# Convolution sums of the vector engine in PSUM, the shifting mean behind the projections, and matmul inputs placed like the weights modulo 128 bytes

## The chip, the cores and the metric

The kernel runs on one core of one Trainium2 chip. The time is that of one execution on the device in microseconds (us); the median of 3 runs is compared. The engines are named as in the profile: PE is TensorE (matmuls; PEld are its weight loads), DVE is VectorE, ACT is ScalarE, POOL is GpSimd, SP issues DMAs.

## The reference

A decoder trunk of two layers over 512 tokens of width 1024, float32. Layer 0 is an mLSTM mixer, layer 1 a Conformer convolution module; each is followed by a gated MLP (width 2816) with a depthwise convolution of three taps. The change sits in layer 1, and in where matmul inputs lie in memory.

```python
def conformer_conv_mixer(x, w_in, b_in, dw_w, dw_b, ln_g, ln_b, w_out, b_out):
    a = x @ w_in + b_in
    u = a[..., :D_MODEL] * jax.nn.sigmoid(a[..., D_MODEL:])
    u = causal_dwconv(u, dw_w, dw_b)          # 31 taps
    u = jax.nn.silu(layernorm(u, ln_g, ln_b))
    return u @ w_out + b_out

def conv_ffn(x, w_up, conv_w, conv_b, w_down):
    hdn = causal_dwconv(x @ w_up, conv_w, conv_b)
    return (jax.nn.silu(hdn[..., :D_FF]) * hdn[..., D_FF:]) @ w_down

def reference(...):
    for i in range(DEPTH):
        h = rmsnorm(x, norm_mix[i])
        x = x + (mlstm_mixer(h, ...) if i % 2 == 0 else conformer_conv_mixer(h, ...))
        x = x + conv_ffn(rmsnorm(x, norm_ffn[i]), ...)
    return rmsnorm(x, norm_final)
```

## The kernel before

Activations lie with channels on the 128 partitions and 512 tokens along the free axis, in 8 blocks of channels. Every float32 operand of a large product is split into two parts of a shorter format, high and low, and a product is done as three matmuls (`mm3`, L160 to L163): high by high, high by low, low by high. Weights come in units of 128x1024: SP loads one (`wr`), ACT writes the high part (`wh`, L149), DVE the low part (`wl`, L150). There are four buffers of `wr` and three each of `wh` and `wl`. A projection of one block is 24 matmuls of 512 columns.

The order on each engine is set when the kernel is built: a scheduler with a timeline of its own places the instructions, and each engine then runs its list strictly in that order. An instruction that waits holds up all that stand behind it on its engine.

A norm's row factor is worked out while the first projections of the next stage run (`norm_finish`, two hooks): a mean over channels on PE (`ms<-ch`, `ms<-cl`, L227 and L228), row values on DVE, the power -0.5 on POOL (`rs`, L232), then DVE spreads it over diagonals (`dgr`, L215) and PE sums those (L218) into all partitions; ACT copies the result to `rsb`. Products are multiplied by `rsb` when they leave PSUM.

In layer 1, `glu(j)` makes two projections for block j of channels (`pa`, `pb`), DVE multiplies both by `rsb` (L717, L718), ACT takes the sigmoid (L719), and DVE forms `u` (L722 or L727). The 31 taps are shared out by block: DVE does blocks 0, 2 and most of 4 (80 taps, `dve_tap`, L744), POOL block 1 and nine taps of 4 (L741, each on a product that ACT makes, L739), and PE blocks 3, 5, 6, 7 with Toeplitz matrices (`conv_pe`, L776). POOL builds those matrices (`toe`, L755; four instructions for each block, two sets of buffers), and DMAs carry `u` and the result to and from PE's layout. DVE's and POOL's taps wait in queues; `background(NV, NG)` takes up to NV and NG of them after each projection.

Then comes the layer norm. All values are shifted by the mean of block 3 (`shift`, giving `kb`), and `stats(j, e)` subtracts `kb` from block j and adds the values and their squares to the sums `s1` and `s2` (L822 to L827). PE sums these over channels (L240), and after the row factors the normalized values go to `zht` and `zlt`, the inputs of the out projection. `PLAN` says after which block which of these runs. PSUM has eight banks of 512 columns: six for `bank()`, two for `small()`.

Of the kernel before, what the change touches and what calls it, by code (L numbers as in the profile page):

```python
# [9 lines left out]
F32 = mybir.dt.float32  # L10
# [4 lines left out]
P = 128  # L15
# [5 lines left out]
NH = 4  # L21
# [5 lines left out]
NEG = -1.0e30  # L27
NPH = 4                    # token phases of the convolution on the tensor engine
NTAU = T // NPH
NJ = (CK + 2 * NPH - 3) // NPH  # L30
GR = 68                    # rows: input gates at 0, running maximum at 32, forget gates at 64

# column offsets in the packed per-channel parameter array
_COLS = {}
# [11 lines left out]
def hybrid_trunk(ctx, tc, x_in, par_in, tph_in, wg_in, wv_in, wqk_in, wo_in, mout_in, cin_in,  # L46
# [6 lines left out]
    wsp = ctx.enter_context(tc.tile_pool(name="wsp", bufs=3))  # L53
    work = ctx.enter_context(tc.tile_pool(name="work", bufs=1))
    psum = ctx.enter_context(tc.tile_pool(name="psum", bufs=6, space=bass.MemoryType.PSUM))
    psms = ctx.enter_context(tc.tile_pool(name="psms", bufs=2, space=bass.MemoryType.PSUM))
# [12 lines left out]

# [1 line left out]
    par = const.tile([P, NPAR], F32, name="par")  # L71
# [22 lines left out]
    def warm(n, after=None):  # L94
        """Products that nobody reads, to keep the clock of the tensor engine up over a wait."""
        ps = bank()
        for _ in range(n):
            with tc.issue_after(after.ins) if after is not None else nullcontext():
                after = PE.matmul(ps[:, :P], ones, ones, start=True, stop=True)  # L99

# [1 line left out]
    seq = []  # L102
# [61 lines left out]

# [1 line left out]
    xh = [None] * KD  # L166
# [31 lines left out]
    def to_rows(src, c, tag):  # L198
        """Values along the free axis, equal on all partitions -> [128 tokens, blocks]."""
        nb = (c.stop - c.start) // P  # L200
        dg = work.tile([P, T], F32, tag="tmp", name=nm("dg"), bufs=4)
        V.tensor_tensor(out=blocks(dg, c), in0=src,
                        in1=ident[:].unsqueeze(1).to_broadcast([P, nb, P]), op=ALU.mult)
        r4 = work.tile([P, NTB], F32, tag=tag, name=nm(tag))
        V.tensor_reduce(out=r4[:, :nb], in_=blocks(dg, c), op=ALU.add, axis=mybir.AxisListType.X)
        return r4

    def from_rows(r4, nb, pb):
        """[128 tokens, blocks] -> the values along the free axis on all partitions (PSUM)."""
        hl = work.tile([P, 2, NTB], F32R, tag="hl", name=nm("hl"))  # L210
        V.tensor_copy(hl[:, 0, :nb], r4[:, :nb])
        V.tensor_tensor(out=hl[:, 1, :nb], in0=r4[:, :nb], in1=hl[:, 0, :nb], op=ALU.subtract)
        for i in range(2):
            dg = work.tile([P, NTB, P], F32R, tag="tmp", name=nm("dgr"), bufs=4)
            v = V.tensor_tensor(out=dg[:, :nb], in0=ident[:].unsqueeze(1).to_broadcast([P, nb, P]),  # L215
                            in1=hl[:, i, :nb].bitcast(F32).unsqueeze(2).to_broadcast([P, nb, P]),
                            op=ALU.mult)
            p = PE.matmul(pb, onesr, dg[:, :nb].rearrange("p a b -> p (a b)"), start=i == 0, stop=i == 1)  # L218
        return v, p

    def col_mean(ps, t, c, w):
        """Sum over the partitions of t times the constant in w, on all partitions."""
        h = work.tile([P, T], F32R, tag="tmp", name=nm("ch"), bufs=4)
        l = work.tile([P, T], F32R, tag="tmp", name=nm("cl"), bufs=4)
        A.copy(h[:, c], t[:, c])
        V.tensor_tensor(out=l[:, c], in0=t[:, c], in1=h[:, c], op=ALU.subtract)
        PE.matmul(ps, w, h[:, c], start=True, stop=False)  # L227
        PE.matmul(ps, w, l[:, c], start=False, stop=True)  # L228
# [6 lines left out]
    def row_sums(ps, t, c, w, start, stop):  # L235
        """Adds the sums over the partitions of t, times w, to ps: [128 tokens, 2 * blocks]."""
        nb = (c.stop - c.start) // P
        for b in range(nb):
            s = slice(c.start + b * P, c.start + (b + 1) * P)
            PE.matmul(ps[:, 2 * b : 2 * b + 2], t[:, s], w[:, :2], start=start and b == 0,  # L240
                      stop=stop and b == nb - 1)

    def norm_rows(nrm, c):
        """1 / rms of the tokens in c, [128 tokens, blocks]."""
        n = c.stop - c.start
# [6 lines left out]

    # the row factors of a norm are worked out between the first products of the next stage
    hooks = []
# [19 lines left out]

    # ================= layer 0: mLSTM =================
    warm(9)
# [47 lines left out]
    VW = DV + 2  # L324
    vh = [mp.tile([P, NTB, VW], F32R, tag=f"vgh{h}", name=f"vh{h}") for h in range(NH)]
    vl = [mp.tile([P, NTB, VW], F32R, tag=f"vgl{h}", name=f"vl{h}") for h in range(NH)]
    for h in range(NH):
# [29 lines left out]

    # gates, channel-major: input gates on partitions 0-3, forget gates on 32-35
    wgh, wgl = next_unit()
# [81 lines left out]
    def att_decay(h):  # L441
        """exp of the decay from s to t less the running maximum; s on partitions, t free."""
        plf, pm = small(), small()
# [147 lines left out]

    # ================= gated MLP with a depthwise convolution =================
    def ffn(l, g=None, last=False):
# [98 lines left out]

    # ================= layer 1: convolution module =================
    cctx = ExitStack()
    cp = cctx.enter_context(tc.tile_pool(name="conv", bufs=1))
    DVE_CH, POOL_CH, PE_CH = (0, 2, 4), (1,), (3, 5, 6, 7)
    NV, NG, NG4, NPRE = 5, 4, 9, 1
    cacc2 = cp.tile([P, T], F32, name="caccp")
# [4 lines left out]
    cacc = {c: cp.tile([P, T], F32, name=f"cacc{c}") for c in range(8)}  # L703
    # 1 where the partition lies in the block of NPH partitions
    tph = cp.tile([P, 8 * 4 * NJ * NPH], F32, name="tph")
# [31 lines left out]
    def pool_tap(j, u, s):  # L737
# [3 lines left out]
        G.tensor_tensor(out=a[:, s:], in0=a[:, s:], in1=p[:, s:], op=ALU.add)  # L741

    def dve_tap(j, u, s):
        V.scalar_tensor_tensor(out=cacc[j][:, s:], in0=u[:, : T - s],  # L744
                               scalar=dw(j, CK - 1 - s), in1=cacc[j][:, s:],
                               op0=ALU.mult, op1=ALU.add)

# [36 lines left out]

    # taps for the vector engine and GpSimd, handed out between the products
    vtaps, gtaps = [], []
# [13 lines left out]
    def shift():  # L800
        """The mean of one block of channels, by which all values are shifted before their sums."""
        d[FIRST] = cp.tile([P, T], F32, name=f"d{FIRST}")
# [10 lines left out]
    def stats(j, e):  # L813
        if j in PE_CH:
# [3 lines left out]
                in0=cacc[j].rearrange("p (q t) -> p t q", q=NPH), scalar=pcol("dw_b", j),  # L818
                in1=kb.rearrange("p (t q) -> p t q", q=NPH), op0=ALU.add, op1=ALU.subtract)
        else:  # L820
            d[j] = cacc[j]
# [9 lines left out]
        5: [lambda: conv_pe(3, *us[3])],  # L831
        6: [shift],
        13: [lambda: stats(1, G)],
        14: [lambda: stats(0, V), lambda: stats(5, V)],
# [3 lines left out]
    for j in range(8):  # L838
# [3 lines left out]
        else:  # L842
            conv_start(j, u)
            if j == 4:
# [7 lines left out]
        for f in PLAN.get(j, ()):  # L852
            f()
    for j in PE_CH[1:]:
        background(2 * NV, 2 * NG)
        conv_pe(j, *us[j])
        for f in PLAN.get(j + 8, ()):
            f()
    background(999, 999)
    G.tensor_tensor(out=cacc[4], in0=cacc[4], in1=cacc2, op=ALU.add)  # L860
    sq4 = stats(4, V)
    sq7 = stats(LAST, None)

    # layer norm over channels
    pr1, pr2, pmu = small(), small(), bank()
# [36 lines left out]
def _layout(inputs):  # L902
    f = {k: np.asarray(v) for k, v in inputs.items()}

    def ch(a):  # [..., C] -> [128, ... * C/128], channel c = m * 128 + p
        a = a.reshape(a.shape[:-1] + (-1, P))
        return np.moveaxis(a, -1, 0).reshape(P, -1)

    def taps(w):  # [K, C] -> [128, C/128 * K]
        k, c = w.shape  # L910
        return w.reshape(k, c // P, P).transpose(2, 1, 0).reshape(P, -1)

    def cols(w, n=P):  # [K, N] -> [N/n, 128, K/128 * n]
        k, c = w.shape
        return w.reshape(k // P, P, c // n, n).transpose(2, 1, 0, 3).reshape(c // n, P, -1)

    # gate biases: input gates on partitions 0-3, forget gates on 32-35
    bg = np.zeros((P, 1), np.float32)
    bg[0:4, 0], bg[32:36, 0] = f["m_b_gates"][0][:4], f["m_b_gates"][0][4:]
    # taps by token phase: dph[c * NPH + p, m, g, j, q] = w[K - 1 - (NPH * j + q - p), m * 128 + g * 32 + c]  # L920
    dw = f["c_dw_w"][0].reshape(CK, KD, 4, P // 4)
# [52 lines left out]
```

## Time and profile before

| | |
|---|---|
| median of 3 runs (lowest, highest) | 1192.71 us (1192.66, 1192.79) |
| span of the profiled execution, first to last instruction | 1191.0 us |
| PE busy, matmuls | 1134.3 us (95%), 5226 |
| DVE busy | 788.6 us (66%), 1022 |
| ACT busy | 510.8 us (43%), 713 |
| POOL busy | 174.8 us (15%), 126 |
| mean granted TensorE clock | 0.974 |

The profiled execution has no time of its own beside its span. The span is 1.7 us below the median, and this is what lies around it in a run. A matmul's duration is that of its whole way through the pipeline; the distance from one start to the next tells how fast PE goes. Busy DVE instructions overlap their neighbours by some 0.08 us where nothing holds them.

### The profile page before, as it was taken

What the parts mean: (1) busy time and instruction counts of PE and PEld (TensorE: products, weight loads), DVE (VectorE), ACT (ScalarE), POOL (GpSimd) and SP (SyncE); (2) the same over time, 40 slices, a digit from 0 to 9 for tenths busy, and PEclk for the clock granted to TensorE, in tenths of its full rate; (3) what the DMA queues carried; (4) which work ended last, traced back from release to release, by engine and by line L of the source; (5) the groups of instructions that cost most, each with busy time, mean ns of one, the idle gap of its engine ahead of it and who ended that gap; (6) DMA issues with size and microseconds to landing.
All of it is one profiled execution on the core that took longest, in us unless ns stands there. A gap on an engine that the chain in (4) does not pass through costs nothing.

```text
span 1191.0 us, 13476 instructions
## 1 busy us (share of the span) xinstructions
PE 1134.3 (95%) x5226; PEld 939.7 (79%) x5226; DVE 788.6 (66%) x1022; ACT 510.8 (43%) x713; POOL 174.8 (15%) x126
## 2 busy tenths in 40 slices
PE   9999999999999999999998757699999999999996
PEld 7788888888888888888887647588888888888886
DVE  6788875487777775332479999874877777752222
ACT  6556774354444443222244522363544444432221
POOL 4000001100000000000267857021000000000002
PEclk9999999999999999999998879699999999999998
DMA  6222123223232323233332112022232323233322
GB/s 247 89 89 71 54 74 103 90 89 106 89 106 89 105 86 92 90 97 98 110 105 62 62 44 67 14 88 89 92 103 90 106 89 106 84 98 89 93 62 71
DMA packets 36369, 106.85 MB, mean 90 GB/s; under 512 B 4049, under 2 KB 10321, under 8 KB 36305
## 3 DMA queue, kind: packets, MB, share of 16 engines
q1 hardware_dynamic: 31728, 103.25, 27.2%
q10 hardware_dynamic: 4576, 2.74, 0.8%
q8 instruction: 41, 0.67, 0.2%
q14 instruction: 24, 0.19, 0.0%
HBM read 101.78 MB, written 2.10 MB: 87 GB/s over the span
## 4 chain that ended last, share of the span: by engine, by line
PE 84%; DVE 13%; issue 1%; ACT 1%; DMA 1%; POOL 0%; ACTq 0%; POOLq 0%; SPq 0%; DVEq 0%
PE mm L161 25%; PE mm L162 25%; PE mm L163 25%; DVE cacc L744 8%; PE mm L580 2%; PE mm L577 2%; PE mm L576 2%; DVE wl L150 2%; PE ms L240 1%; PE mm L99 0%; DMA xall<-in_dram 0%; PE ms L218 0%; DVE u L722 0%; DVE se L453 0%; DVE s L826 0%
## 5 line engine op out<-in xcount | busy, mean ns | idle before, releaser
L163 PE MATMUL mm<-xh,wl 128*128 128x512 f32 x960 | 375.6, 391 | 3.3 <-DVE wl L150 3.3
L161 PE MATMUL mm<-xh,wh 128*128 128x512 f32 x960 | 375.6, 392 | 0.0
L162 PE MATMUL mm<-xl,wh 128*128 128x512 f32 x960 | 375.4, 391 | 0.0
L150 DVE TENSOR_TENSOR wl<-wr,wh 128x1024 fp32r<-128x1024 f32 (+1 forms) x192 | 236.5, 1235 | 165.5 <-ACT wh L149 163.3
L149 ACT CAST wh<-wr 128x1024 fp32r<-128x1024 f32 (+1 forms) x192 | 197.4, 1030 | 296.1 <-PE mm L162 243.6
L163 PEld LDWEIGHTS mm<-xh,wl 128*128 128x128 f32 x960 | 181.4, 189 | 41.9 <-DVE wl L150 3.7
L162 PEld LDWEIGHTS mm<-xl,wh 128*128 128x128 f32 x960 | 181.4, 189 | 37.9
L161 PEld LDWEIGHTS mm<-xh,wh 128*128 128x128 f32 x960 | 181.5, 189 | 37.2
L193 POOL TENSOR_TENSOR acc<-acc,sq 128x512 f32<-128x512 f32 x30 | 43.3, 1444 | 746.7 <-ACT sq L191 746.2
L161 PE MATMUL mm<-yh,wh 128*128 128x512 f32 (+1 forms) x374 | 142.3, 380 | 0.0
L162 PE MATMUL mm<-yl,wh 128*128 128x512 f32 (+1 forms) x374 | 142.3, 380 | 0.0
L163 PE MATMUL mm<-yh,wl 128*128 128x512 f32 (+1 forms) x374 | 142.2, 380 | 0.0
L606 DVE TENSOR_TENSOR mm<-mm,rsb 128x512 f32<-128x512 f32 x88 | 60.8, 695 | 76.0 <-PE mm L163 73.1
L744 DVE SCALAR_TENSOR_TENSOR cacc<-u,par,cacc 128x501 f32<-128x501 f32 (+27 forms) x80 | 102.1, 1321 | 0.1
L161 PEld LDWEIGHTS mm<-yh,wh 128*128 128x128 f32 x374 | 70.0, 187 | 15.5
L162 PEld LDWEIGHTS mm<-yl,wh 128*128 128x128 f32 x374 | 70.0, 187 | 15.3
L163 PEld LDWEIGHTS mm<-yh,wl 128*128 128x128 f32 x374 | 70.0, 187 | 15.2
L616 ACT CAST yh<-ta 128x512 fp32r<-128x512 f32 x44 | 27.3, 620 | 104.6 <-DVE ta L615 104.6
L611 DVE SCALAR_TENSOR_TENSOR ta<-mm,par,ta 128x511 f32<-128x511 f32 x88 | 65.6, 745 | 1.3
L611 DVE SCALAR_TENSOR_TENSOR tb<-mm,par,tb 128x511 f32<-128x511 f32 x88 | 65.5, 746 | 1.4
L614 ACT ACTIVATE ta<-ta 128x512 f32<-128x512 f32 x44 | 27.8, 632 | 79.4 <-DVE ta L611 79.4
L741 POOL TENSOR_TENSOR cacc<-cacc,cprod 128x511 f32<-128x511 f32 (+29 forms) x30 | 49.5, 1651 | 24.1 <-ACT cprod L739 22.4
(237 smaller groups left out, 1200.5 us busy)
## 6 DMA issues: line engine op xcount, KB each, us to landing
wr<-in_dram SPq DMA_DIRECT2D x175, 512.0 KB, 3.5
wr<-in_dram SPq DMA_DIRECT2D x16, 384.0 KB, 3.1
xall<-in_dram SPq DMA_DIRECT2D x8, 256.0 KB, 6.4
us<-u ACTq DMA_DIRECT2D x16, 64.0 KB, 2.1
out_dram<-xall SPq DMA_DIRECT2D x2, 384.0 KB, 3.5
tph<-in_dram SPq DMA_DIRECT2D x1, 576.0 KB, 4.5
wr<-in_dram SPq DMA_DIRECT2D x2, 256.0 KB, 3.9
cacc<-co ACTq DMA_DIRECT2D x8, 64.0 KB, 2.4
```

The lines of the kernel that those rows point to most:

```text
L149: st["last"] = A.copy(hi[:, :n], r[:, :n])
L150: V.tensor_tensor(out=lo[:, :n], in0=r[:, :n], in1=hi[:, :n], op=ALU.subtract)
L161: PE.matmul(ps, lh, rh, start=start, stop=False)
L162: PE.matmul(ps, lh, rl, start=False, stop=False)
L163: PE.matmul(ps, ll, rh, start=False, stop=stop)
L193: e.tensor_tensor(out=nrm.acc[:, c], in0=nrm.acc[:, c], in1=sq[:, c], op=ALU.add)
L606: V.tensor_tensor(out=ps, in0=ps, in1=rs["b"], op=ALU.mult)
L611: V.scalar_tensor_tensor(out=t[:, s:], in0=ps[:, : T - s], scalar=pcol("fconv_w", m * 3 + 2 - s), in1=t[:, s:], op0=ALU.mult, op1=ALU.add)
L614: A.activation(ta, ta, AF.Silu)
L616: A.copy(yh[:, j, :], ta)
L741: G.tensor_tensor(out=a[:, s:], in0=a[:, s:], in1=p[:, s:], op=ALU.add)
L744: V.scalar_tensor_tensor(out=cacc[j][:, s:], in0=u[:, : T - s], scalar=dw(j, CK - 1 - s), in1=cacc[j][:, s:], op0=ALU.mult, op1=ALU.add)
```

## The change

Four things change; all else in the diff is comments.

1. `dve_tap` accumulates in a PSUM bank. At a block's first tap a bank is taken and ACT writes the first term there; after the last one ACT copies the sum to `cacc[j]` (for block 4, DVE's `stats` reads the bank and adds `cacc2`, from which POOL has taken `kb` before). In a tap one input is `u` in SBUF, the other and the output are in the bank. NV is 4, not 5.
2. `shift` goes from after block 6 to after block 7, with POOL's `stats(1)`; `conv_pe(5)` comes up from behind the projections to after block 6.
3. A tile `pad` of 64 bytes stands at the head of the pool `work`, which moves every tile behind it.
4. The mLSTM's `v` tiles, whose places the mixer's outputs take over later, are made 96 bytes longer.

In the built program, tiles start at these bytes of a partition modulo 128. Weights `wh` and `wl`, and the norm outputs `xh` and `xl`: 64 before and after. The MLP's `yh` and `yl`, and the layer norm's `zht` and `zlt`: 0 before, 64 after. The mixer's `gh` and `gl`: 0, 32, 64 and 96 for heads 0 to 3 before, 64 for all after. Modulo 512 they agree less: the weights are at 64, `yh` and `yl` go from 256 to 320, `zht` and `zlt` from 128 to 192.

```diff
-    DVE_CH, POOL_CH, PE_CH = (0, 2, 4), (1,), (3, 5, 6, 7)
-    NV, NG, NG4, NPRE = 5, 4, 9, 1
+    NV, NG, NG4, NPRE = 4, 4, 9, 1
...
+    work.tile([P, 16], F32, name="pad")
...
-    vh = [mp.tile([P, NTB, VW], F32R, tag=f"vgh{h}", name=f"vh{h}") for h in range(NH)]
+    def v_tile(what, h):
+        t = mp.tile([P, NTB * VW + 24], F32R, tag=f"vg{what}{h}", name=f"v{what}{h}")
+        return t[:, : NTB * VW].rearrange("p (a b) -> p a b", a=NTB)
+    vh = [v_tile("h", h) for h in range(NH)]
...
+    pacc = {}
+
     def dve_tap(j, u, s):
-        V.scalar_tensor_tensor(out=cacc[j][:, s:], in0=u[:, : T - s],
-                               scalar=dw(j, CK - 1 - s), in1=cacc[j][:, s:],
-                               op0=ALU.mult, op1=ALU.add)
+        if j not in pacc:
+            pacc[j] = bank()
+            A.activation(pacc[j], u, AF.Identity, scale=dw(j, CK - 1), bias=pcol("dw_b", j))
+        a = pacc[j]
+        V.scalar_tensor_tensor(out=a[:, s:], in0=u[:, : T - s], scalar=dw(j, CK - 1 - s),
+                               in1=a[:, s:], op0=ALU.mult, op1=ALU.add)
+        if s == CK - 1 and j != 4:
+            A.copy(cacc[j], a)
...
+        elif j == 4:
+            d[j] = cacc[j]
+            V.tensor_tensor(out=d[j], in0=pacc[j], in1=cacc2, op=ALU.add)
...
         5: [lambda: conv_pe(3, *us[3])],
-        6: [shift],
-        13: [lambda: stats(1, G)],
+        6: [lambda: conv_pe(5, *us[5])],
+        7: [shift, lambda: stats(1, G)],
...
-    for j in PE_CH[1:]:
+    for j in PE_CH[2:]:
...
-    G.tensor_tensor(out=cacc[4], in0=cacc[4], in1=cacc2, op=ALU.add)
+    G.tensor_tensor(out=cacc2, in0=cacc2, in1=kb, op=ALU.subtract)
```

The change also moves instructions that the diff doesn't name, since the scheduler places them anew. The first place is on PE, at the row factor of layer 1's first norm. Before, its two products (L218) stand in the projection of `pa` of block 2 (the bank `mm_4713`), after five whole projections:

```order
L162 MATMUL mm_4713<-xl_387_4399,wh_4661 128x512
L218 MATMUL ms_4592<-dgr_4596,onesr 128x512
L163 MATMUL mm_4713<-xh_386_4398,wl_4662 128x512
L161 MATMUL mm_4713<-xh_390_4491,wh_4661 128x512
L218 MATMUL ms_4592<-dgr_4599,onesr 128x512
```

Now the same two (L220) stand between the last matmul of block 0 (bank `mm_4524`) and the first of block 1 (bank `mm_4623`):

```order
L164 MATMUL mm_4524<-xl_391_4493,wh_4527 128x512
L165 MATMUL mm_4524<-xh_390_4492,wl_4528 128x512
L220 MATMUL ms_4593<-dgr_4597,onesr 128x512
L220 MATMUL ms_4593<-dgr_4600,onesr 128x512
L163 MATMUL mm_4623<-xh_362_3842,wh_4571 128x512
```

They come up by 68 rows of 512 columns; the product `ms<-ch` of the same norm keeps its place, and the first of the two stands 12 rows behind it. On POOL, which makes the operand of that step, the order is the same as before: eight Toeplitz instructions, then `rs`.

```order
L779 MEMSET us_5112 128x4x8
L770 TENSOR_TENSOR toe_4902<-msk_4518,tph 128x1152 x4
L770 TENSOR_TENSOR toe_5118<-msk_4518,tph 128x1152 x4
L234 TENSOR_TENSOR rs_400_4561<-ms_399_4558,mhalf 128x4
L748 TENSOR_TENSOR cacc_4509<-cacc_4509,cprod_4700 128x511
```

Nothing has moved there; DVE's `dgr` still needs `rs`, and `rs` still stands behind both sets of `toe`.

The second place is the end of the projections on PE. Before, the mean's two products (L227, L228) stand around the first matmul of `pa` of block 7 (`mm_5304`):

```order
L163 MATMUL mm_5194<-xh_390_4491,wl_5198 128x512
L227 MATMUL ms_5293<-ch_5294,pdvr 128x512
L161 MATMUL mm_5304<-xh_362_3841,wh_5241 128x512
L228 MATMUL ms_5293<-cl_5295,pdvr 128x512
L162 MATMUL mm_5304<-xl_363_3842,wh_5241 128x512
```

Now the mean (L229, L230) stands behind the last matmul of the last projection (bank `mm_5328`), ahead of the convolutions of blocks 6 and 7 (L791):

```order
L164 MATMUL mm_5328<-xl_391_4493,wh_5331 128x512
L165 MATMUL mm_5328<-xh_390_4492,wl_5332 128x512
L229 MATMUL ms_5417<-ch_5418,pdvr 128x512
L230 MATMUL ms_5417<-cl_5419,pdvr 128x512
L791 MATMUL mm_5443<-us_5266,toe_5272 128x128 x18
L791 MATMUL mm_5466<-us_5266,toe_5272 128x128 x18
L791 MATMUL mm_5508<-us_5399,toe_5405 128x128 x18
```

The convolution of block 5 has gone from behind these to between blocks 6 and 7, so only two are left here. On DVE the taps of blocks 0, 2 and 4 were interleaved before, up to three sums at a time; now each sum is done nearly to its end before the next begins, so that most taps follow a tap on the same bank. Behind the last product of the projections (multiplied at L724, `mm_5328`) stand 32 rows of DVE: 12 taps of block 4, the subtraction of `kb` and the sums of all blocks, one `wl`, and `u` of block 7.

```order
L724 TENSOR_TENSOR mm_5328<-mm_5328,rsb_4603 128x512
L758 SCALAR_TENSOR_TENSOR mm_5433<-u_5008,par,mm_5433 128x493
L152 TENSOR_TENSOR wl_5689<-wr_5363,wh_5688 128x1024
L824 TENSOR_TENSOR d_5415<-d_5415,kb 128x512
L840 TENSOR_TENSOR cacc_4508<-cacc_4508,kb 128x512
L831 SCALAR_TENSOR_TENSOR d_5494<-cacc_4513,par,kb 128x512
L758 SCALAR_TENSOR_TENSOR mm_5433<-u_5008,par,mm_5433 128x492
L840 TENSOR_TENSOR cacc_4510<-cacc_4510,kb 128x512
L729 SCALAR_TENSOR_TENSOR u_5397<-mm_5327,par,sg_5393 128x128x4
```

Before, `kb` was subtracted and the sums were begun while projections and convolutions still ran; now none of it can begin until the last projection is through.

## Rows read from the trace of the kernel before

**Rows 1.** Busy time by stretch: start:end, length, engines with (count), PEclk, DMA share, GB/s.

```profile
640.00:758.00 118.00, 73.85 (x435) 64.72 (x433) 117.97 (x107) 39.33 (x61) 76.63 (x45) 0.82 0.20 58
```

**Rows 2.** Who waited for whom, 600 to 770 us: total us, times, longest us.

```profile
PE mm L776 <- DMA us<-u: 8.5, 3, 3.7
...
PE ms L227 <- ACT ch L225: 6.6, 1, 6.6
...
PE mm L163 <- DVE wl L150: 3.3, 1, 3.3
```

**Rows 3.** Timeline of PE: start us, us, what, [idle before <-releaser].

```profile
697.52 0.79 PE L228 MATMUL ms<-cl,pdvr 128*128 128x512 f32 x1 [14.16 <-DVE cl L226]
698.11 0.63 PE L162 MATMUL mm<-xl,wh 128*128 128x512 f32 x1
...
701.95 0.52 PE L162 MATMUL mm<-xl,wh 128*128 128x512 f32 x1
...
712.53 8.28 PE L776 MATMUL mm<-us,toe 128*128 128x128 f32 x72 [1.65 <-DMA us<-u]
...
757.49 3.58 PE L240 MATMUL ms<-invd,s 128*128 128x2 f32 x16 [11.65 <-DVE s L826]
```

**Rows 4.** DVE instructions by line: count, duration ns min/median/max, first and last start, forms.

```profile
L744 DVE SCALAR_TENSOR_TENSOR cacc<-u,par,cacc x80: 705/1400/2596, 619.8 to 751.4; 128x501 f32<-128x501 f32 x3, 128x500 f32<-128x500 f32 x3, 128x499 f32<-128x499 f32 x3, 128x498 f32<-128x498 f32 x3
...
L518 DVE SCALAR_TENSOR_TENSOR mm<-mm,par,sig x8: 746/750/759, 112.6 to 180.0; 128x512 f32<-128x512 f32 x8
...
L717 DVE TENSOR_TENSOR mm<-mm,rsb x8: 684/685/699, 612.5 to 722.8; 128x512 f32<-128x512 f32 x8
```

**Rows 5.** Timeline of DVE, pieces of 619 to 758 us.

```profile
619.82 1.53 DVE L744 SCALAR_TENSOR_TENSOR cacc<-u,par,cacc 128x511 f32<-128x511 f32 x2
...
698.63 0.72 DVE L744 SCALAR_TENSOR_TENSOR cacc<-u,par,cacc 128x494 f32<-128x494 f32 x1
699.27 1.22 DVE L150 TENSOR_TENSOR wl<-wr,wh 128x1024 fp32r<-128x1024 f32 x1
...
752.78 1.64 DVE L826 TENSOR_TENSOR s<-s,cacc 128x512 f32<-128x512 f32 x1
754.35 0.68 DVE L827 TENSOR_TENSOR s<-s,csq 128x512 f32<-128x512 f32 x1
```

**Rows 6.** Groups of 610 to 790 us: count | busy us, mean ns of one | idle before.

```profile
L150 DVE TENSOR_TENSOR wl<-wr,wh 128x1024 fp32r<-128x1024 f32 x16 | 23.0, 1443 | 0.0
...
L816 DVE SCALAR_TENSOR_TENSOR d<-cacc,par,kb 128x512 f32<-128x512 f32 x3 | 3.3, 1095 | 0.0
```

**Rows 7.** Timeline of 588 to 613 us, engine in each row.

```profile
588.78 19.67 POOL L755 TENSOR_TENSOR toe<-msk,tph 128x1152 f32<-128x1152 f32 x8 [4.24 <-DMA tph<-in_dram]
...
592.60 0.39 PE L227 MATMUL ms<-ch,invdr 128*128 128x512 f32 x1
...
609.46 0.17 DVE L211 CAST hl<-rs 128x4 fp32r<-128x4 f32 x1 [5.08 <-POOL rs L232]
...
609.74 1.29 DVE L215 TENSOR_TENSOR dgr<-ident,hl 128x512 fp32r<-128x512 f32 x2
...
612.50 0.70 DVE L717 TENSOR_TENSOR mm<-mm,rsb 128x512 f32<-128x512 f32 x1 [0.34 <-ACT rsb L269]
```

**Rows 8.** Timeline of PE, first and last matmul of two runs without gaps.

```profile
249.96 0.39 PE L161 MATMUL mm<-xh,wh 128*128 128x512 f32 x1
...
253.36 0.39 PE L161 MATMUL mm<-xh,wh 128*128 128x512 f32 x1
...
519.79 0.39 PE L162 MATMUL mm<-yl,wh 128*128 128x512 f32 x1
...
525.39 0.39 PE L162 MATMUL mm<-yl,wh 128*128 128x512 f32 x1
```

**Rows 9.** Chain that ended last, both out projections: start us, us, what.

```profile
190.79 1.87 PE mm L580 x8
...
786.17 1.83 PE mm L580 x8
```

More of the change, by code (lines that the diff above doesn't have):

```diff
@@ L324, in hybrid_trunk @@
     VW = DV + 2
-    vh = [mp.tile([P, NTB, VW], F32R, tag=f"vgh{h}", name=f"vh{h}") for h in range(NH)]
-    vl = [mp.tile([P, NTB, VW], F32R, tag=f"vgl{h}", name=f"vl{h}") for h in range(NH)]
+    def v_tile(what, h):
+        t = mp.tile([P, NTB * VW + 24], F32R, tag=f"vg{what}{h}", name=f"v{what}{h}")
+        return t[:, : NTB * VW].rearrange("p (a b) -> p a b", a=NTB)
+    vh = [v_tile("h", h) for h in range(NH)]
+    vl = [v_tile("l", h) for h in range(NH)]
     for h in range(NH):
@@ L842, in hybrid_trunk @@
         else:
-            conv_start(j, u)
+            if j in POOL_CH:
+                conv_start(j, u)
             if j == 4:
```

## The prediction, made before the changed kernel ran

> **What bounds the kernel now.** I first looked at busy time by stretch. Almost everywhere PE works without a break; the exception is the convolution module. From 640 to 758 us PE is busy 73.85 us of 118, so it idles 44 us, while DVE is busy all 118 [rows 1]. Only there can less work on DVE shorten the run; elsewhere only a faster PE can. Then I asked who waited. PE waited 14.16 us for `cl`, the low part of the mean's input, which stood in DVE's list behind taps, 6.6 us for the high part, 3.3 us for a weight's low part, 8.5 us in all for shuffled `u`, and 11.65 us at the end for DVE's sums [rows 2, 3]. After the 14.16 us the next matmuls start 0.427 us apart instead of 0.227, ten of them from 698.11 to 701.95 [rows 3]: PE's clock had fallen, and each long stop costs some 2.0 us more.
>
> **DVE's taps.** A tap takes 705 ns at the least, but 1400 in the median and up to 2596 [rows 4]. Its two tensor inputs are both in SBUF. The multiplication by `rsb`, with one input and the output in PSUM, takes 684 to 699 ns, though it runs between the same taps and beside the same POOL work [rows 4]. So what stretches the taps strikes instructions with two SBUF inputs while POOL works; the plain sum at L826 with 1.64 us against 0.68 in the row behind shows the same [rows 5]. A tap with `u` in SBUF and the sum in PSUM has one SBUF input only. The nearest row for its own duration is L518, the same operation on 512 columns into PSUM: 750 ns [rows 4].
>
> What of a tap's duration counts is the distance between starts. A tap followed by something else takes 0.64 us (698.63 to 699.27); two taps in a row on one sum take 1.53, some 0.78 each [rows 5]. By the new order 41 taps follow one on the same bank and 39 don't: with shortening columns 41 x 0.77 + 39 x 0.65 = 57 us. The 80 now take 80 x 1.32 = 106 (the page's mean of L744), so DVE is relieved of some 45 us.
>
> [...]
>
> **A new stop at the start.** The scheduler has moved the row factor's products up to 12 rows behind `ms<-ch`. That one starts at 592.60, so PE is there at 592.60 + 12 x 0.227 = 595.3. But `dgr` needs `rs`, and on POOL `rs` stands, as before, behind eight Toeplitz instructions that last from 588.78 to 608.45; `dgr` ends at 609.74 + 1.29 = 611.03 [rows 7]. Before, PE had projections to do until then. Now it stands still for about 15.7 us, and the clock falls. PE goes on at about 611.5, and `rsb` comes as before, near 612.5.
>
> **PE from there.** 14 projections at 24 x 0.2267 = 5.44 us are 76.2 us; the convolutions of blocks 3 and 5 at 8.3 us each [rows 3] are 16.6; the slow clock costs 2.0. The last projection ends at 611.5 + 76.2 + 16.6 + 2.0 = 706.3. DVE must keep up with the `wl` of each unit: from 612.5 up to its 32 rows behind the last projection it has 79 us of work (68 taps, 15 products by `rsb`, 13 `wl` at 1.14, seven `u`, `cl`), 2 us for the first sigmoid and 3 to 6 for `wl` stretched by POOL (mean 1.44 us against 1.22 alone [rows 5, 6]). That makes 612.5 + 79 + 7 = 698.5, ahead of PE. `wl` of `pb` in block 2, the tightest, comes about 626.5, when PE needs it at about 630.
>
> **The tail.** Behind the last projection DVE has 32 rows: 12 taps at 0.70 (8.4), ten sums at 0.60, four subtractions at 0.61, three shifted reads like L816 at 1.01 (1.095 less the overlap [rows 6]), `u` 1.04, `wl` 1.13 and a product 0.61: 22.7 us. POOL subtracts and sums beside it for some 8 us, which stretches about three of these by 1 us, as at L826. DVE's sum of values, next to last, is done at 706.3 + 22.1 + 3 = 731.4, and PE can begin the sums over channels. The convolutions of blocks 6 and 7 end near 706.3 + 0.5 + 16.6 + 1 = 724.4 and are hidden. Before, PE began those sums at 757.49 [rows 3]: 26.1 us. In this I left out every wait between engines inside the projections; before there was one of 3.3 us [rows 2], and I take off 3 for such. The module gives back 23 us. Its two parts are not separable by addition: the mean's 20.8 us of waiting goes, but PE needs DVE's faster taps to use that time, and the new stop takes 15.7 of it.
>
> The bounds. If POOL stretches all 19 two-SBUF instructions of the tail and the projections slip by 6, 14 us remain; with neither, and a stop shorter by 1 us because one `wl` less disturbs POOL, it is 30.
>
> **The placement.** In the up projections 15 matmuls take 253.36 - 249.96 = 3.40 us, 226.7 ns each; in the down projection 24 take 525.39 - 519.79 = 5.60, 233.3 each [rows 8]. PE is never short of work in either. The weights are the same kind; the moving input lies at 64 modulo 128, like the weights, in the first, and at 0 in the second. In the out projections eight matmuls take 1.87 us (inputs at 0 to 96) and 1.83 (at 0) [rows 9], 233 and 229 ns. So the place of the input goes with the pace, but 0 modulo 128 gives 233 in one stage and 229 in another, where modulo 512 it is 256 and 128. After, all agree modulo 128 but not modulo 512. No row shows a long run like this. Bounds: nothing, and all at 226.7. The down projections have 528 + 462 = 990 matmuls of 512 columns, 6.6 ns each: 6.5 us; the out projections 192 x 6 and 192 x 2.4 ns: 1.6 us. I take 7 of these 8.1, nearer the row whose inputs agree.
>
> **The sum.** Span 1191.0 - 23 - 7 = 1161.0, and 1.7 around it: 1162.7 us. The other edits cost nothing that counts: ACT's two copies out of PSUM and three first terms replace three first terms that it wrote before, and ACT is busy 39 us of 118 [rows 1]; one bank less for projections matters only if PE gets more than two blocks ahead, which the late `rsb` allows it once, during the stop. If ACT or the banks were late, `wl` or the sigmoid would be, and PE would stop; that is the third rival.
>
> **Rivals.**
> - Main case, as summed: 50%, range 1155 to 1171.
> - The placement gives nothing, because the pace hangs on more than the remainder modulo 128 (228 and 233 at the same 0 speak for it): 1162.7 + 7 = 1170. 22%. [...]
> - The projections run at a pace set by others: ACT's products for POOL, POOL's taps and the casts stand in one list with the sigmoids, and block 1's taps now start some 15 us later. If each of 12 projections waits 1 us, the module gives 11 us: 1175. 16%. Against it: each `wl` and sigmoid stands some 3 us or more ahead of its use.
> - The stop isn't there, since `dgr` comes early or PE has gone slower anyway: PE is up to 15 us ahead, and DVE sets the end at 612.5 + 101 + 5 + 2: 8 to 10 us less, 1153. 6%. `rs` behind `toe` speaks against it.
> - Slower: taps in PSUM are as slow as those in SBUF, because POOL's work holds up their read of `u` too. Then DVE has 80 x 0.6 = 50 us more, the tail begins at DVE's pace, and the sums at 612.5 + 2 + 101 + 5 + 50 = 770 instead of 757.5: 1192.7 + 13 - 7 = 1199. It decides from a mean distance of taps of about 1.0 us. 6%; the 684 to 699 ns of L717 speak against it.
>
> A measurement of this kernel can tell about 0.2%, 2.4 us, from no change. Only the last case is slower: 0.05; a mixture near it gives 0.02 for the same; faster 0.93. The range takes in the first three cases and the edge of the fourth: 1152 to 1180.
>
> **What would show it.** Taps at 710 to 760 ns with little spread. A wait of PE of 14 to 16 us before the row factor's product, on DVE's `dgr`, with slow matmuls behind it. No wait at the mean's products. PE's sums over channels about 26 us earlier, still waiting for DVE. Down projections at 227 ns. Wrong it would be if taps spread up to 1.6 us, if PE waits at each projection for ACT or DVE, or if `yh` still goes at 233.

## The result and the profile after

The changed kernel takes 1171.53 us (1170.79 to 1171.67, 4 runs), the kernel before beside it 1192.75. The ratio is 0.982, with an interval from 0.9806 to 0.9834: 21.2 us less. The profiled execution has a span of 1169.1 us and took 1170.79. The forecast was 1162.7 us with a range of 1152 to 1180; the time lies 8.8 us above the forecast and inside the range.

Four places of the trace say where this comes from. First the taps. The view of one line's instructions (count, duration ns min/median/max, first and last start, forms), changed kernel:

```profile
L758 DVE SCALAR_TENSOR_TENSOR mm<-u,par,mm x80: 711/732/755, 611.9 to 732.6; 128x501 f32<-128x501 f32 x3, 128x500 f32<-128x500 f32 x3, 128x499 f32<-128x499 f32 x3, 128x498 f32<-128x498 f32 x3
```

Against [rows 4] the median has fallen from 1400 to 732 ns and the spread is gone, though POOL works as before: 74.85 us in the 118 us below, against 76.63. Busy time by stretch, the same 118 us as in [rows 1]:

```profile
640.00:758.00 118.00, 102.67 (x579) 90.79 (x578) 93.06 (x128) 55.55 (x83) 74.85 (x50) 0.90 0.23 67
```

PE does 102.7 us of work in this stretch instead of 73.9, and DVE is no longer busy all the time. The module ends earlier now, so the last 21 us of the stretch belong to what stands behind it. Then the waits of PE, which answer to [rows 2] (whole program here):

```profile
PE ms L220 <- DVE dgr L217: 16.4, 3, 14.2
PE mm L791 <- DMA us<-u: 8.0, 1, 8.0
PE ms L242 <- DVE s L844: 4.9, 1, 4.9
PE mm L165 <- DVE wl L152: 1.5, 1, 1.5
```

The waits for the mean are gone. In their place stand a stop of 14.2 us at the row factor and one of 8.0 us for a shuffled `u`. The timeline of PE shows both (start us, us, what, idle before):

```profile
591.64 0.39 PE L165 MATMUL mm<-xh,wl 128*128 128x512 f32 x1
606.23 1.40 PE L220 MATMUL ms<-dgr,onesr 128*128 128x512 f32 x2 [14.20 <-DVE dgr L217]
607.42 0.63 PE L163 MATMUL mm<-xh,wh 128*128 128x512 f32 x1
...
705.60 0.40 PE L229 MATMUL ms<-ch,pdvr 128*128 128x512 f32 x1
...
706.06 8.20 PE L791 MATMUL mm<-us,toe 128*128 128x128 f32 x72
722.30 10.11 PE L791 MATMUL mm<-us,toe 128*128 128x128 f32 x72 [8.04 <-DMA us<-u]
737.27 1.86 PE L242 MATMUL ms<-invd,s 128*128 128x2 f32 x8 [4.86 <-DVE s L844]
```

The last projection is done at 705.60. Block 6 is convolved at once, block 7 only from 722.30, and the sums over channels begin at 737.27, where [rows 3] have 757.49. Why so late stands in DVE's timeline behind the projections:

```profile
688.92 2.37 DVE L152 TENSOR_TENSOR wl<-wr,wh 128x1024 fp32r<-128x1024 f32 x1 [5.19 <-ACT wh L151]
...
703.69 3.08 DVE L758 SCALAR_TENSOR_TENSOR mm<-u,par,mm 128x501 f32<-128x501 f32 x4 [7.05 <-ACT mm L756]
...
711.43 0.69 DVE L724 TENSOR_TENSOR mm<-mm,rsb 128x512 f32<-128x512 f32 x1
712.03 0.73 DVE L758 SCALAR_TENSOR_TENSOR mm<-u,par,mm 128x493 f32<-128x493 f32 x1
712.67 2.19 DVE L152 TENSOR_TENSOR wl<-wr,wh 128x1024 fp32r<-128x1024 f32 x1
714.78 0.68 DVE L824 TENSOR_TENSOR d<-d,kb 128x512 f32<-128x512 f32 x1
715.38 0.68 DVE L840 TENSOR_TENSOR cacc<-cacc,kb 128x512 f32<-128x512 f32 x1
715.98 1.37 DVE L831 SCALAR_TENSOR_TENSOR d<-cacc,par,kb 128x512 f32<-128x512 f32 x1
...
717.91 1.08 DVE L840 TENSOR_TENSOR cacc<-cacc,kb 128x512 f32<-128x512 f32 x1
718.92 1.10 DVE L729 SCALAR_TENSOR_TENSOR u<-mm,par,sg 128x512 f32<-128x512 f32 x1
...
735.53 1.09 DVE L831 SCALAR_TENSOR_TENSOR d<-cacc,par,kb 128x512 f32<-128x512 f32 x1 [1.50 <-DMA cacc<-co]
736.54 0.68 DVE L844 TENSOR_TENSOR s<-s,cacc 128x512 f32<-128x512 f32 x1
```

Twice DVE has nothing to do, 5.2 and 7.05 us. Both times it waits for ACT, the second time for block 4's first term, which ACT writes into PSUM only at 702.87 us (timeline of ACT):

```profile
702.87 0.78 ACT L756 ACTIVATE mm<-u,par 128x512 f32<-128x512 f32 x1 [0.69 <-ACT co L795]
```

Then everything comes at once: block 4's taps, two low parts of weights, four differences from the mean, and behind them, at 718.92, the `u` of block 7, for which PE stands.

Last the placement. Two matmuls of the down projection, 24 apart, in the timeline of PE:

```profile
514.74 0.39 PE L164 MATMUL mm<-yl,wh 128*128 128x512 f32 x1
...
520.18 0.39 PE L164 MATMUL mm<-yl,wh 128*128 128x512 f32 x1
```

5.44 us, 226.7 ns each, against 233.3 in [rows 8]. In the second out projection the chain of waits has eight matmuls in 1.87 us, against 1.83 in [rows 9]: there it got slower.

```profile
766.16 1.87 PE mm L587 x8
```

### The profile page after: what moved, and what is told of

It is laid out like the page before. It is cut to its first block, busy times and chain, and to the rows that moved or that the text cites. A ratio compares the mean times of both kernels' runs of the same rounds, so it can differ in the third digit from the quotient of the medians.

```text
span 1169.1 us, 13465 instructions
## 1 busy us (share of the span) xinstructions
PE 1127.0 (96%) x5226; PEld 939.6 (80%) x5226; DVE 748.1 (64%) x1022; ACT 512.3 (44%) x715; POOL 164.3 (14%) x126
## 4 chain that ended last, share of the span: by engine, by line
PE 83%; DVE 5%; POOL 5%; ACT 2%; DMA 2%; issue 1%; ACTq 0%; POOLq 0%; SPq 0%; DVEq 0%
PE mm L164 25%; PE mm L163 25%; PE mm L165 25%; POOL toe L770 2%; POOL cacc L748 2%; DVE mm L758 2%; PE mm L587 2%; PE mm L584 2%; PE mm L583 2%; PE mm L791 1%; DVE wl L152 1%; POOL caccp L748 1%; PE ms L242 1%; ACT cprod L746 0%; DMA tph<-in_dram 0%
## 5 line engine op out<-in xcount | busy, mean ns | idle before, releaser
L758 DVE SCALAR_TENSOR_TENSOR mm<-u,par,mm 128x501 f32<-128x501 f32 (+15 forms) x80 | 58.5, 734 | 9.3 <-ACT mm L756 7.9
L748 POOL TENSOR_TENSOR cacc<-cacc,cprod 128x511 f32<-128x511 f32 (+29 forms) x30 | 44.3, 1477 | 29.7 <-ACT cprod L746 27.7
```

The source lines that it names most:

```text
L758: V.scalar_tensor_tensor(out=a[:, s:], in0=u[:, : T - s], scalar=dw(j, CK - 1 - s), in1=a[:, s:], op0=ALU.mult, op1=ALU.add)
```

## The experiments

Twelve kernels ran, each timed in turn with the kernel before. Times are medians. They ran in three sets, and the kernel before took 1192.7 to 1194.1 us beside them, so the ratio is what to compare.

| kernel | us | before beside it | ratio, interval |
|---|---|---|---|
| changed kernel | 1171.53 | 1192.75 | 0.982 (0.9806 to 0.9834) |
| place_only | 1187.58 | 1192.82 | 0.9953 (0.9935 to 0.9971) |
| sbuf_taps | 1200.15 | 1192.82 | 1.0056 (1.0040 to 1.0072) |
| psum_only | 1169.91 | 1192.69 | 0.9806 (0.9791 to 0.9821) |
| psum_place | 1166.26 | 1194.10 | 0.9764 (0.9750 to 0.9779) |
| pad192 | 1175.57 | 1192.69 | 0.9859 (0.9842 to 0.9875) |
| w128 | 1191.14 | 1194.10 | 0.9977 (0.9968 to 0.9987) |
| nv5 | 1166.36 | 1192.82 | 0.9773 (0.9758 to 0.9789) |
| rs_first | 1167.66 | 1192.82 | 0.9781 (0.9765 to 0.9796) |
| toe_late | 1160.95 | 1192.69 | 0.9733 (0.9718 to 0.9747) |
| best3 | 1148.72 | 1192.69 | 0.9628 (0.9613 to 0.9642) |
| best4 | 1153.82 | 1194.10 | 0.9666 (0.9648 to 0.9684) |
| best4n5 | 1150.63 | 1194.10 | 0.9640 (0.9625 to 0.9654) |

My theory after the result was that taps, move and placement each help, and that the module fell short by its tail. The main rival: one part costs time, and another gives more than I thought.

### The parts one by one

**place_only.** The kernel before with the padding alone:

```diff
+    work.tile([P, 16], F32, name="pad")
+        t = mp.tile([P, NTB * VW + 24], F32R, tag=f"vg{what}{h}", name=f"v{what}{h}")
```

> The kernel before with only the padding ahead of the work tiles and in the value tiles; taps, mean and order of the work as before. Theory A (the pace of a matmul follows the place of its moving input, and both down projections fall from 233.3 to 226.8 ns a matmul while the second out projection gets slower, 229 to 233): 990 x 6.5 ns less 0.8 us, so 1187.0 us (1186 to 1188). Rival (the 8.1 us of the forecast, out projections included): 1184.6. Rival (the whole gain of the change lies in the convolution module): 1192.7.

5.2 us, as theory A has it within the measurement. The second out projection goes at some 232 ns a matmul (26 in 6.03 us, from 790.96 us on in the timeline of PE) instead of 229.

**sbuf_taps.** The changed kernel, with the sums back in SBUF:

```diff
-            pacc[j] = bank()
+            pacc[j] = cacc[j]
-        if s == CK - 1 and j != 4:
-            A.copy(cacc[j], a)
```

> The changed kernel with DVE's sums back in SBUF (no first term into PSUM, no copies out of it); the mean stays behind the projections and the placement stays. Theory A (DVE sets the end of the convolution module, the mean's wait was only where its lateness showed): taps spread up to 2 us again, DVE has some 45 us more work, and only the placement and little else is left of the gain: 1187 us (1183 to 1192). Rival (moving the mean takes its 20.8 us of PE waits away by itself): 1172 to 1176. Rival (taps cost the same in SBUF): 1171.5.

All of the gain is lost, and more: 1200.15 us, 12.6 above place_only. Its taps by line, its waits of PE, and DVE where the mean is due:

```profile
L758 DVE SCALAR_TENSOR_TENSOR cacc<-u,par,cacc x80: 701/1665/2592, 616.5 to 747.8; 128x501 f32<-128x501 f32 x3, 128x500 f32<-128x500 f32 x3, 128x499 f32<-128x499 f32 x3, 128x498 f32<-128x498 f32 x3
```

```profile
PE mm L789 <- DMA us<-u: 31.4, 2, 17.3
PE ms L230 <- DVE cl L228: 14.4, 1, 14.4
PE ms L229 <- ACT ch L227: 7.0, 1, 7.0
```

```profile
675.39 18.12 DVE L758 SCALAR_TENSOR_TENSOR cacc<-u,par,cacc 128x498 f32<-128x498 f32 x12
693.44 0.68 DVE L228 TENSOR_TENSOR cl<-d,ch 128x512 fp32r<-128x512 f32 x1
```

Twelve taps take 18 us, 1.5 each, and `cl` stands behind them. The mean is behind the projections here, and PE still waits 21 us for it. So the move does not take these waits away. That the time went above that of before was in no theory. PE waits 31.4 us for shuffled `u`, where place_only has 7.0, so the move itself seemed to cost; but the two also differ in the number of taps handed out (four and five) and in block 4's sum.

**psum_only.** The kernel before with the sums in PSUM and four taps at a time; the mean and the placement stay. The edit is that part of the change's diff: `pacc`, `dve_tap`, block 4's sum, and `NV`.

> The kernel before with DVE's sums in PSUM (and four taps at a time) only: the mean stays between the projections, no padding. Theory A (the two parts of the module are not separate: with short taps the mean's low part comes sooner, but still behind taps, and the 14 us stop at the row factor is there): 1186 us (1182 to 1190). Rival (with short taps the place of the mean costs nothing): 1177. Rival (the taps' relief is worth nothing without the move): 1193 or more.

All three missed: 1169.91 us. This part alone gives 22.8 us, as much as the whole change; the two intervals overlap. Its waits at the mean, in the timeline of PE:

```profile
691.50 0.50 PE L227 MATMUL ms<-ch,pdvr 128*128 128x512 f32 x1 [1.47 <-ACT ch L225]
...
695.76 0.80 PE L228 MATMUL ms<-cl,pdvr 128*128 128x512 f32 x1 [2.61 <-DVE cl L226]
...
736.85 1.87 PE L240 MATMUL ms<-invd,d 128*128 128x2 f32 x8 [2.25 <-DVE d L824]
```

The 20.8 us have become 4.1 without any move. The stop at the row factor is here too (13.9 us). In place_only and sbuf_taps PE waits for `dgr` 2.0 us at most, so the stop comes with the sums in PSUM, not with the placement, the move or the four taps. And DVE does the differences early, before it has the `u` of block 7 to make:

```profile
699.86 1.29 DVE L817 TENSOR_TENSOR d<-d,kb 128x512 f32<-128x512 f32 x1
701.07 3.47 DVE L833 TENSOR_TENSOR cacc<-cacc,kb 128x512 f32<-128x512 f32 x2
...
715.01 1.12 DVE L722 SCALAR_TENSOR_TENSOR u<-mm,par,sg 128x512 f32<-128x512 f32 x1
```

**psum_place.** The two parts together, that is, the changed kernel without the move of the mean:

> The kernel before with the sums in PSUM and with the padding, the mean left between the projections: the changed kernel without the move of the mean. Theory A (the parts add: sums in PSUM gave 22.8 us alone, the padding 5.2 alone, so moving the mean costs the changed kernel 6.8 us, because all that needs the mean then stands behind the last projection): 1164.7 us (1163.5 to 1166). Rival (the move costs nothing once the placement is there): 1170 to 1172.

0.9764 of 1192.75 is 1164.6 us, the sum of the two parts. The change with the move stands at 0.982, and the intervals don't touch. Moving the mean, with the new place of block 5's convolution that belongs to it, costs the changed kernel some 6.7 us by the ratios and 5.3 by the medians.

### What remains: the stop and the tail

**rs_first.** Toeplitz work on POOL is queued behind the row factor's power:

```diff
+            with tc.issue_after(st["rs"].ins):
                 G.tensor_tensor(out=toe[:, g]...
```

> The changed kernel with the Toeplitz instructions of POOL queued behind the row factor's power, so that the row factor comes some 10 us earlier. Theory A (the 14.4 us stop of PE and the slow matmuls behind it are on the path, and DVE starts its taps earlier by the same 10 us): the stop shrinks below 6 us and the time falls by 9 to 13: 1160.5 us (1158 to 1163). Rival (DVE's list or ACT's sets the end, so PE's time is lost again at later waits): 1167 to 1171.

Only 3.9 us by the medians: the rival's number, but not shown to be for its reason, since PE's stop did not shrink below 6 us as theory A had it (6.9 us are left for the first diagonal). The power came at 593.87, but in the timelines of POOL and DVE the next steps hang:

```profile
593.87 1.02 POOL L234 TENSOR_TENSOR rs<-ms,mhalf 128x4 f32<-128x4 f32 x1 [11.09 <-DVE ms L251]
594.86 10.24 POOL L771 TENSOR_TENSOR toe<-msk,tph 128x1152 f32<-128x1152 f32 x4
```

```profile
595.82 2.09 DVE L213 CAST hl<-rs 128x4 fp32r<-128x4 f32 x1
597.94 2.04 DVE L214 TENSOR_TENSOR hl<-rs,hl 128x4 fp32r<-128x4 f32 x1
599.91 3.21 DVE L217 TENSOR_TENSOR dgr<-ident,hl 128x512 fp32r<-128x512 f32 x2
```

Four elements a partition take 2.09 us on DVE, 0.17 in [rows 7]; a Toeplitz instruction beside them lasts 10.24 / 4 = 2.6 us.

**toe_late.** So the mask that the Toeplitz instructions read is made behind the diagonals:

```diff
     def toeplitz(j):
+        if j == FIRST:
+            with tc.issue_after(st["dgr"].ins):
+                V.tensor_reduce(out=msk4[:, :, 0], ...
```

> The changed kernel with the mask of the Toeplitz instructions made behind the row factor's diagonals on DVE, so that POOL's Toeplitz work starts only when these are done. Theory A (with the Toeplitz instructions right behind the power, DVE's two tiny instructions of the row factor took 2.0 us each and a diagonal 2.6, because POOL's work held them up; without it they take 0.2 and 0.7): PE goes on 4 to 5 us earlier than there, and the time is 1163.5 us (1162 to 1165). Rival (the end is set by DVE's list and the chain of block 7, which don't start earlier for it): 1167 to 1168.

1160.95 us, 10.6 below the changed kernel and 1 us below theory A's range. DVE:

```profile
594.14 0.16 DVE L213 CAST hl<-rs 128x4 fp32r<-128x4 f32 x1
...
594.42 1.28 DVE L217 TENSOR_TENSOR dgr<-ident,hl 128x512 fp32r<-128x512 f32 x2
```

The stop of 14.2 us was on the path nearly in full; 3.1 us of it remain.

**nv5.** Five taps at a time instead of four (`NV = 5`), so that block 4 starts earlier:

> The changed kernel with five DVE taps (before: four) handed out at each projection, so that block 4's first term and taps come ahead of blocks 6 and 7. Theory A (DVE stood idle about 12 us from 684 to 704 because block 4's first term came late on ACT, and its 17 taps then lengthened the tail): the tail gets 3 to 6 us shorter: 1167 us (1165 to 1169). Rival (the chain u of block 7, shuffle, convolution, copy back sets the end): 1170 to 1171.5. Rival (more taps ahead of the weights' low parts make PE wait in the projections): above 1172.

5.2 us, as theory A had it. Block 7 now sets the end, as the rival had it, but only behind this gain. The timeline of PE:

```profile
723.25 9.97 PE L791 MATMUL mm<-us,toe 128*128 128x128 f32 x72 [7.78 <-DMA us<-u]
733.06 1.84 PE L242 MATMUL ms<-invd,s 128*128 128x2 f32 x16
737.49 0.80 PE L242 MATMUL ms<-invd,d 128*128 128x2 f32 x3 [2.58 <-DVE d L831]
```

The sums `s` of the other blocks are ready earlier now, at 733.06; the difference of block 7 is not.

### The placement

**pad192.** 192 bytes of padding instead of 64 (`work.tile([P, 48], ...)`):

> The changed kernel with 192 bytes of padding ahead of the work tiles in place of 64: the inputs of the down projections then lie at 64 modulo 128, like the weights, but at 192 modulo 256, and those of the second out projection at 64 modulo 256. Theory A (what counts is the place modulo 256: after the change 64 and 320 modulo 512 go at 226.8 ns, 192 and 448 at 232 to 233): down projections 5.5 ns slower, second out projection 6.5 ns faster, 990 x 5.5 less 192 x 6.5 ns: 1175.7 us (1175 to 1177). Rival (what counts is agreement modulo 128, as the change has it): down projections as they are: 1170.3 to 1171.5.

4.0 us slower than the changed kernel, as theory A says. 24 matmuls of the down projection:

```profile
514.76 0.39 PE L163 MATMUL mm<-yh,wh 128*128 128x512 f32 x1
...
520.37 0.39 PE L163 MATMUL mm<-yh,wh 128*128 128x512 f32 x1
```

5.61 us, 233.8 ns each, though the input agrees with the weights modulo 128.

**w128.** The weights moved instead:

```diff
+    wsp.tile([P, 32], F32, name="wpad", bufs=1)
-    work.tile([P, 16], F32, name="pad")
+    work.tile([P, 48], F32, name="pad")
```

> The changed kernel with the split weights moved by 128 bytes (to 192 modulo 256), the x inputs left at 64 modulo 256 and those of the down projections kept at 64 modulo 256 by more padding. Theory A (what counts is that moving input and weights have the same remainder modulo 256): about 3,500 matmuls on the path slow from 226.8 to 232 or 233 ns, 20 us: 1191 us (1187 to 1196). Rival (what counts is the moving input's own place, whatever the weights'): 1171.5 (1170 to 1173).

Theory A. Nothing about the x inputs was changed, and their matmuls, 226.7 ns before, take 232.0 (15 in 3.48 us). The inputs of the second out projection lie at 192 modulo 256 here, like the moved weights, and take 226.7 (15 in 3.40 us):

```profile
309.67 0.39 PE L164 MATMUL mm<-xh,wh 128*128 128x512 f32 x1
...
313.15 0.39 PE L164 MATMUL mm<-xh,wh 128*128 128x512 f32 x1
...
777.85 0.39 PE L584 MATMUL mm<-zht,wh 128*128 128x512 f32 x1
...
781.25 0.39 PE L585 MATMUL mm<-zlt,wh 128*128 128x512 f32 x1
```

So what counts in these runs is not the place of either but that both have the same remainder modulo 256. That it is 256 and not 512 rests on the down projections of the changed kernel, which go at 226.7 ns with inputs at 320 modulo 512 and weights at 64.

### Together

**best3** is the changed kernel with toe_late, nv5, 128 bytes more ahead of the second out projection's inputs, and the differences queued behind the last `u` (`with tc.issue_after(st["u"].ins)` around them in `stats`):

> The changed kernel with four things together: Toeplitz work behind the row factor's diagonals, five taps at a time, the last block's u ahead of the differences on DVE, and 128 bytes more ahead of the second out projection's inputs (64 modulo 256). Theory A (each takes away a wait on the path: 8 us at the row factor, 5 for five taps, 3 to 4 for u, 1.2 for the place): 1153 us (1150 to 1158). Rival (the waits hide one another, DVE's list then sets the end): 1160 to 1163.

1148.72 us, 22.8 below the changed kernel and 1.3 below theory A's range. It is the fastest version that ran, but best4n5 is no slower by any difference that the intervals tell. The late differences have no run of their own. PE still waits 6.6 us for the shuffled `u` of block 7:

```profile
PE mm L795 <- DMA us<-u: 6.6, 1, 6.6
PE ms L220 <- DVE dgr L217: 5.3, 3, 3.1
```

**best4** and **best4n5** have the same edits on psum_place, where the mean is between the projections, with four taps at a time and with five.

> The mean between the projections, sums in PSUM, four taps at a time, padding, Toeplitz work behind the row factor's diagonals, the last block's u ahead of the differences, second out projection's inputs at 64 modulo 256. Theory A (10.6 us at the row factor and 1.2 at the place, off the 1164.7 expected for the version without the move): 1152.5 us (1150 to 1155). Rival (DVE, which runs without a break from the last projection on, takes back what PE gains): 1157 to 1161.

> The version that took 1148.7 us (all four edits, five taps at a time) with the mean back between the projections; nothing else differs. Theory A (behind the projections the mean costs some 7 us in any version, since the differences and sums of five blocks wait for it): 1143 us (1141 to 1146). Rival (with u ahead of the differences and block 4 done early the move costs nothing, and earlier mean products only make PE wait for DVE): 1148 to 1152.

best4 gives what theory A expected, by its ratio 1152.9 us. best4n5 gives the rival: 0.9640, and 0.9628 for best3, whose intervals overlap. The place of the mean costs some 6.7 us in the changed kernel and nothing that can be told in this version.

## Why the forecast was right and where it was off

**DVE's taps** was right. Taps with one SBUF input have a median of 732 ns, beside the forecast 710 to 760. With two they have 1400 before and 1665 in sbuf_taps, yet a single one takes 0.72 us at 698.63 [rows 5], while POOL stands idle (693.12 to 699.63). By what means POOL's work stretches them was not shown. The rival of slow taps in PSUM is out.

**A new stop at the start** was right: 14.2 us at `dgr` against 15.7 in the sum, and 607.42 when the projections go on. The matmuls behind it are slow, as forecast: they start 0.43 us apart from 607.42 to 609.98 us, at a granted clock of 0.50 there. In the kernel before it was 0.50 too, from 697.5 to 702 us. toe_late shows its price, 10.6 us.

**PE from there** was right to a few us. The module began 3.5 us earlier (`ms<-ch` at 589.10 instead of 592.60), so 706.3 stands for 702.8 here; the last projection ended at 705.60. The 3 us that I took off for slips are about this; 1.5 of them are the wait for `wl` in the view above.

**The tail** failed, and at its start. I had 25.1 us from the last projection to the channel sums; it was 737.27 - 705.60 = 31.7. The 32 rows themselves took what the sum gave them: the first tap of them starts at 712.03 and the sum of values ends at 736.54 + 0.68 = 737.22, 25.2 us. But I let them begin with the end of the projections, because DVE would be done with all else at 698.5, "ahead of PE". It multiplied the last product only at 711.43: it had stood idle 12.2 us for ACT, and so 17 taps were left behind the last projection and not 12. Part of this is ACT's late first term, whose cost I had put at nothing ("ACT's two copies ... and three first terms replace three first terms"). My third rival had ACT's list setting the pace; it came in on DVE's side, not as waits of PE in each projection. nv5, which brings the first term earlier, gives 5.2 us back.

A second sentence was wrong: "the convolutions of blocks 6 and 7 end near 724.4 and are hidden". Block 7's `u` stood behind four differences and two low parts on DVE, and its convolution ended at 732.4. On DVE's list that is the wait of 1.50 us at 735.53, small beside the late start. How much the late `u` costs by itself was not measured alone.

"The mean's 20.8 us of waiting goes" was true of the trace, but the step that gave the credit to the move failed. Sums in PSUM alone give 22.8 us and leave 4.1 us of the mean's waits; the move then costs some 6.7. The traces suggest why: the differences and sums that need the mean all come behind the last projection, on the engine that is late there. That the parts don't add holds, but not as I had it: what the move costs depends on the rest, 6.7 us here and nothing in best3. The module as a whole gave 592.60 to 757.49 less 589.10 to 737.27, 16.7 us instead of 23. The lower bound of 14 does not follow from its own terms: with 1 us for each of the 16 instructions beyond the three already in the sum, and 6 for slips, it is 26.1 - 16 - 6 = 4.

**The placement** was mis-sized, 5.2 us instead of 7. The down projections gave what the sum had (6.6 ns a matmul). The out projections gave nothing: remainders modulo 128 were the wrong ones to look at, and the second went from 128 to 192 modulo 256, from 229 ns to 232 in place_only and 233 in the changed kernel (24 in 5.60 us, from 779.07 us on). (The 228 among the rivals is the 229 of [rows 9].) w128 slows the matmuls of the x inputs from 226.7 to 232.0 ns each by moving nothing but buffers in SBUF; why was not tested.

6.3 us less from the module and 1.8 less from behind it (433.5 against 431.8 us, where 3.5 were due) make the 8.1 us by which the span missed.

## What to carry to other kernels

When one part of a change removes the cause of a wait, don't give the credit to another part that moves the waiter: ask what the wait would be with the first part alone. Work that is put behind the last matmul of a stage joins a queue there, so list that queue row by row, with the inputs that PE still needs at its end. Before a long POOL instruction is placed, look at the smallest DVE instruction that something waits for: if they overlap, the small one can get as slow as the cast of rs_first, which took 2.09 us beside a Toeplitz instruction of 2.6, and 0.16 without one in toe_late.

## What was not expected of the hardware

In these runs a matmul of 512 columns went at 226.7 ns where its moving input and its weights had the same remainder modulo 256 bytes in SBUF (64 in the down projections of the changed kernel, 192 in the second out projection of w128). In the other pairs that occurred it took 229 to 234: 233.8 with the input at 192 and the weights at 64 (pad192), 232.0 the other way round (w128), 229 with 128 and 64 and 233.3 with 0 and 64 (both before). A cast of four elements a partition on DVE took 2.09 us beside POOL's Toeplitz instruction (rs_first) and 0.16 without it (toe_late).
